# First norm of a two-layer hybrid: another order of VectorE's and ScalarE's first work, half of the squares on VectorE

## The chip, the core and the metric

One core of a Trainium2 chip runs the whole program. Its engines have queues of their own: TensorE (PE) multiplies, VectorE (DVE) and ScalarE (ACT) work elementwise, GpSimd (POOL) does a few copies, SyncE (SP) issues most DMAs. An engine takes its instructions in the order of its queue; where one waits for another engine or for a DMA, all behind it wait too. The metric is the device time of one execution in microseconds; less is better.

## The reference, cut to what matters

Two layers on a sequence of 512 tokens of width 1024, batch 1. The first is dilated attention, the second an mLSTM, each followed by a SwiGLU; a norm stands ahead of each and at the end. What this document deals with is the very beginning: the first norm and the rotary angles.

```
def rms_norm(x, g):
    xf = x.astype(jnp.float32)
    y = xf * lax.rsqrt(jnp.mean(xf * xf, axis=-1, keepdims=True) + RMS_EPS)
    return y.astype(x.dtype) * g.astype(x.dtype)

def apply_partial_rope(t, positions):
    ang = positions.astype(jnp.float32)[..., None] * inv_freq
    cos = jnp.cos(ang)[:, :, None, :]
    sin = jnp.sin(ang)[:, :, None, :]
...
h = x
h = h + dilated_attention_mixer(rms_norm(h, attn_norm[0]), positions, attn_w_in[0], attn_w_out[0])
...
proj = (xn @ w_in).reshape(B, S, N_GROUPS, 3, ATTN_HEADS, ATTN_HEAD_DIM)
```

## The kernel before

All activations are kept transposed: 128 features on the partitions, 512 tokens along a row, so x is eight tiles of 128 x 512 (KC = 8). Every matrix product is done in three passes: both operands are split into a high half, rounded to a shorter float (written by ScalarE), and a low half, the remainder (written by VectorE), and high x high, high x low and low x high are added up (SPLITS). So each tile of weights or activations costs ScalarE one instruction and VectorE one ahead of TensorE.

The norm's factor per token is not applied ahead of the first products: the products run on x times the gain, and the result is multiplied by the factor when it is taken out of PSUM. The factor's way is: squares of x summed per token (`squares`, two halves `hf` of 512 features with TB = 4 blocks of 128 tokens each, results in `ss2`), their sum `xv` (L504), a Newton inverse root, eight small diagonal blocks `xdg` (L323), and two matmuls `xbc` (L329) that spread it over the partitions. `xrbc` (L330) is that factor in SBUF; all evacuations of queries and keys need it.

The start is laid out by hand, from about L340 to L530:

- On SyncE's queue, x and the first weights come in five pieces of 1, 1, 2, 2 and 2 of the eight tiles (`pieces`), x and weights in turn, then constants, then the next weights (`a0g0k`, `a0g1q`) as their buffers come free. The positions and the gains come through ScalarE's queue.
- `x_piece(i)` splits the weights of a piece (`first_split`: `first_h` L443 on ScalarE, `first_l` L444 on VectorE), and for each tile of it transposes x on TensorE (`x_in`, `xT` L305) and splits the result times the gain (`xa_h` L226 on ScalarE, `xa_l` L227 on VectorE).
- `first_mm(i)` are the matmuls of piece i of the first product, `a0g0q` (L454).
- `gains` transposes the gains on TensorE (`arT` L428) and copies them into `cols` on VectorE (L429); every `xa_h` and `xa_l` reads them.
- `rope_turns` (L366 to L372) makes angles out of the positions on VectorE: a memset, four casts of one row each, a shuffle, two scalings. `rope_angles` (L375 to L378) reduces them to one turn. `rope_tables` takes two sines on ScalarE (L381, L382), three small steps on VectorE (L383 to L385) and eight copies on GpSimd into `sinn` and `cosn`.
- `x_keep(k)` copies the transposed x out of PSUM into `h` for the residual (VectorE for k < 4, L433; ScalarE for the rest, L435) and so frees its bank.
- `next_weights(ch)` splits the two chunks of the second product's weights (`a0g0k_k_h` L208, `a0g0k_k_l` L209).
- `idle(n)` are matmuls on ones whose result is not used; eight of them run at the start (L107).

The order on each engine is forced with `tc.issue_after(ins)`: what is traced in it goes behind `ins` in the queue of `ins`'s engine. `behind(fn, engine=E)` puts what `fn` issues on E behind E's last instruction so far (TensorE when no engine is named); `both` does it for VectorE and ScalarE at once. Where nothing is forced, the framework's scheduler settles the order when the program is built, by its own reckoning of when operands are ready; so the matmuls inside one `first_mm`, and the place of `xbc` among the matmuls of the second product `a0g0k` (L239), are its choice. `xbc` is traced after the first half of `a0g0k`.

Buffers: the tags "v" and "vf" have one buffer each; "vf" holds the angles (`tmp`) first and values later. The banks of the transposed x are handed to `a0g0k` and to the third product `a0g1q` when `x_keep` has read them.

Of the kernel before, what the change touches and what calls it, by code (L numbers as in the profile page):

```python
# [11 lines left out]
F32 = mybir.dt.float32  # L12
F32R = mybir.dt.float32r
I32 = mybir.dt.int32
AF = mybir.ActivationFunctionType
ALU = mybir.AluOpType
AX = mybir.AxisListType
P = 128
# [52 lines left out]
def tile_hybrid_dilated_attn_mlstm(  # L71
# [4 lines left out]
    nc = tc.nc  # L76
# [3 lines left out]
    def pool(stack, name, **kw):  # L80
        return stack.enter_context(tc.tile_pool(name=name, bufs=1, **kw))
# [75 lines left out]
    def last_on(engine):  # L157
        for ins in reversed(nc.cur_bb.bb.instructions):
            if ins.engine == engine:
                return ins  # L160
# [184 lines left out]
    with ExitStack() as actx:  # L345
        ap = pool(actx, "attn")
# [5 lines left out]
        part = lambda at, w: acst[:, at - K_MA:at - K_MA + w]  # L352
# [11 lines left out]
        def rope_turns():  # L364

            nc.vector.memset(n, 0.0)  # L366
            for c in range(4):
                s = slice(32 * c, 32 * c + 1)
                nc.vector.tensor_copy(n[s], posi[s].rearrange("p (j c) -> p c j", c=4)[:, c])
            nc.vector.stream_shuffle(ang, n, [0] * 32)  # L370
            nc.vector.tensor_scalar(ang, ang, cst[:, K_INV:K_INV + 1], None, op0=ALU.mult)
            nc.vector.tensor_scalar(n, ang, 1.0 / TWO_PI, ROUND, op0=ALU.mult, op1=ALU.add)  # L372
# [22 lines left out]
        xtok = ap.tile([P, TB, D], F32, tag="heads", name="x_tok")  # L395
# [18 lines left out]
        def behind(fn, *args, engine=mybir.EngineType.PE):  # L414

            with tc.issue_after(last_on(engine)):
                fn(*args)
# [40 lines left out]
        ss2 = ap.tile([P, 2, TB], F32, name="x_ss")  # L458

        def squares(hf):  # L460
            for tb in range(TB):
                sq = ap.tile([P, 512], F32, tag="v", name="x_sq")
                nc.scalar.activation(sq, xtok[:, tb, hf * 512:(hf + 1) * 512], AF.Square,
                                     accum_out=ss2[:, hf, tb:tb + 1])

        ACT, DVE = mybir.EngineType.Activation, mybir.EngineType.DVE

        def both(fn, *args):
            with tc.issue_after(last_on(ACT)):
                behind(fn, *args, engine=DVE)  # L470

        rope_turns()
        with tc.issue_after(last_on(DVE)):
            behind(gains)

        def x_piece(i):
            both(first_split, i)
            k, n = pieces[i]
            for kk in range(k, k + n):
                with tc.issue_after(last_on(ACT)), tc.issue_after(last_on(DVE)):  # L480
                    behind(x_in, kk)
        x_piece(0)
        x_piece(1)
        behind(first_mm, 0)
        x_piece(2)
        behind(first_mm, 1)
        both(x_keep, 0)
        both(x_keep, 1)
        behind(rope_angles, engine=DVE)
        x_piece(3)  # L490
        behind(first_mm, 2)
        both(rope_tables)
        both(x_keep, 2)
        both(x_keep, 3)
        x_piece(4)
        behind(squares, 0, engine=ACT)
        behind(first_mm, 3)
        def next_weights(ch):
            ready.append(split_chunk(weight_chunk(w_in, ch, D, 4, "a0g0k_k%d" % ch)))
        both(next_weights, 0)  # L500
        behind(squares, 1, engine=ACT)
        both(next_weights, 1)
        v = npl.tile([P, TB], F32, tag="rs_v4", name="xv", bufs=2)
        nc.vector.tensor_tensor(v, ss2[:, 0], ss2[:, 1], op=ALU.add)  # L504
# [632 lines left out]
    with ExitStack() as mctx:  # L1137
# [101 lines left out]
        for b in range(TB):  # L1239
            ve.scalar_tensor_tensor(fblk[32 * b:32 * b + H], blk(lf)[:, b], bias2[:, 1:2], blk(t0)[:, b],  # L1240
                                    op0=ALU.add, op1=ALU.add)
# [174 lines left out]
    with ExitStack() as fctx:  # L1416
# [47 lines left out]
        for n in range(2):  # L1464
# [27 lines left out]
            for at, tb, cs in tiles:  # L1492
# [10 lines left out]
                part = 0 if n == 0 else 1 if cs.stop < 512 else 2  # L1503
                nc.scalar.activation(junk[:, cs], t, AF.Square, accum_out=fss[:, tb, part:part + 1])
                if part == (1 if tb == TB - 1 else 0):
                    nc.vector.tensor_tensor(fpre[:, tb:tb + 1], fss[:, tb, 0:1], fss[:, tb, 1:2], op=ALU.add)
                    nc.vector.tensor_scalar(fpre[:, tb:tb + 1], fpre[:, tb:tb + 1], 1.0 / D, EPS,
                                            op0=ALU.mult, op1=ALU.add)
                nc.gpsimd.tensor_tensor(t, t, gbc[:, n * 512 + cs.start:n * 512 + cs.stop], op=ALU.mult)
                if n == 1 and cs.stop == 512:  # L1510

                    v = fv[:, tb:tb + 1]
                    nc.vector.scalar_tensor_tensor(v, fss[:, tb, 2:3], 1.0 / D, fpre[:, tb:tb + 1],
                                                   op0=ALU.mult, op1=ALU.add)
# [35 lines left out]
```

## Time and profile before

| | |
|---|---|
| median of 3 runs | 1429.59 us (1429.14 to 1430.78) |
| the profiled execution | 1429.9 us |
| its span, first to last instruction | 1427.3 us |
| mean granted TensorE clock | 0.998 |
| PE / DVE / ACT / POOL busy | 99% / 67% / 42% / 6% of the span |

A page of the profile gives busy times by engine, queues, and groups of instructions; the trace behind it can be asked for the waits of an engine, for a timeline, and for groups by line. Times in these views count from the span's start. The profiled execution is one run; the difference of 2.6 us between its time and its span lies outside its instructions.

### The profile page before, as it was taken

What the parts mean: (1) busy time and instruction counts of PE and PEld (TensorE: products, weight loads), DVE (VectorE), ACT (ScalarE), POOL (GpSimd) and SP (SyncE); (2) the same over time, 40 slices, a digit from 0 to 9 for tenths busy, and PEclk for the clock granted to TensorE, in tenths of its full rate; (3) what the DMA queues carried; (4) which work ended last, traced back from release to release, by engine and by line L of the source; (5) the groups of instructions that cost most, each with busy time, mean ns of one, the idle gap of its engine ahead of it and who ended that gap; (6) DMA issues with size and microseconds to landing.
All of it is one profiled execution on the core that took longest, in us unless ns stands there. A gap on an engine that the chain in (4) does not pass through costs nothing. (4 is left out here: it accounts for less than half of the span.)

```text
span 1427.3 us, 20249 instructions
## 1 busy us (share of the span) xinstructions
PE 1415.0 (99%) x7980; PEld 1240.0 (87%) x7980; DVE 960.3 (67%) x1680; ACT 604.1 (42%) x1010; POOL 84.9 (6%) x136
## 2 busy tenths in 40 slices
PE   8999999999999999999999999999999999999998
PEld 6888888888888888999998888888888899999887
DVE  7857557567567397787772358897758778788233
ACT  5333224224225353544462233696534354445123
POOL 1011011011002000000000010110000000002001
PEclk9999999999999999999999999999999999999999
DMA  6346236335335434323232332322133332335331
GB/s 193 102 114 202 76 104 188 100 106 153 133 104 144 146 102 133 106 73 118 90 96 96 96 98 74 104 60 60 52 113 96 125 118 83 96 119 178 118 106 72
DMA packets 134215, 158.65 MB, mean 111 GB/s; under 512 B 7076, under 2 KB 121572, under 8 KB 134120
## 3 DMA queue, kind: packets, MB, share of 16 engines
q1 hardware_dynamic: 126160, 131.55, 29.7%
q0 software_dynamic: 6288, 24.68, 6.1%
q8 instruction: 62, 1.02, 0.3%
q10 hardware_dynamic: 1672, 1.13, 0.2%
q14 instruction: 33, 0.27, 0.1%
HBM read 143.18 MB, written 14.16 MB: 110 GB/s over the span
## 5 line engine op out<-in xcount | busy, mean ns | idle before, releaser
L1479 PE MATMUL fin<-fw_l,f1hh 128*128 128x512 f32 (+1 forms) x198 | 72.5, 366 | 0.0
L1479 PE MATMUL fin<-fw_h,f1hh 128*128 128x512 f32 (+1 forms) x198 | 72.4, 366 | 0.0
L1479 PE MATMUL fin<-fw_h,f1hl 128*128 128x512 f32 (+1 forms) x198 | 72.4, 365 | 0.0
L209 DVE TENSOR_TENSOR fo_k_l<-fo_k_w,fo_k_h 128x1024 fp32r<-128x1024 f32 (+1 forms) x24 | 27.2, 1133 | 62.0 <-ACT fo_k_h L208 62.0
L239 PE MATMUL fo<-f0hh,fo_k_h 128*128 128x512 f32 x176 | 68.5, 389 | 0.0
L239 PE MATMUL fo<-f0hl,fo_k_h 128*128 128x512 f32 x176 | 68.5, 389 | 0.0
L239 PE MATMUL fo<-f0hh,fo_k_l 128*128 128x512 f32 x176 | 68.5, 389 | 0.0
L209 DVE TENSOR_TENSOR fw_l<-fw_w,fw_h 128x1024 fp32r<-128x1024 f32 x22 | 27.0, 1230 | 59.9 <-ACT fw_h L208 59.9
L208 ACT ACTIVATE fo_k_h<-fo_k_w 128x1024 fp32r<-128x1024 f32 (+1 forms) x24 | 23.7, 989 | 74.7 <-PE fo L239 74.7
L208 ACT ACTIVATE fw_h<-fw_w 128x1024 fp32r<-128x1024 f32 x22 | 23.3, 1060 | 67.3 <-PE fin L1479 67.0
L1479 PEld LDWEIGHTS fin<-fw_l,f1hh 128*128 128x128 f32 x198 | 37.4, 189 | 6.2 <-DVE fw_l L209 0.2
L1479 PEld LDWEIGHTS fin<-fw_h,f1hh 128*128 128x128 f32 x198 | 37.4, 189 | 6.2
L1479 PEld LDWEIGHTS fin<-fw_h,f1hl 128*128 128x128 f32 x198 | 37.3, 189 | 6.0
L239 PEld LDWEIGHTS fo<-f0hh,fo_k_h 128*128 128x128 f32 x176 | 33.0, 188 | 6.9
L239 PEld LDWEIGHTS fo<-f0hl,fo_k_h 128*128 128x128 f32 x176 | 33.0, 188 | 6.9
L239 PEld LDWEIGHTS fo<-f0hh,fo_k_l 128*128 128x128 f32 x176 | 33.0, 188 | 6.7
L239 PE MATMUL f0j<-n_h,f0j_h 128*128 128x512 f32 x96 | 37.5, 390 | 0.0
L239 PE MATMUL f1j<-n_h,f1j_h 128*128 128x512 f32 x96 | 37.5, 390 | 0.0
L239 PE MATMUL f0j<-n_h,f0j_l 128*128 128x512 f32 x96 | 37.4, 389 | 0.0
L239 PE MATMUL f1j<-n_h,f1j_l 128*128 128x512 f32 x96 | 37.4, 389 | 0.0
L239 PE MATMUL f0j<-n_l,f0j_h 128*128 128x512 f32 x96 | 37.3, 389 | 0.0
L239 PE MATMUL f1j<-n_l,f1j_h 128*128 128x512 f32 x96 | 37.3, 389 | 0.0
(2104 smaller groups left out, 4879.5 us busy)
## 6 DMA issues: line engine op xcount, KB each, us to landing
f0j_w<-in_ffn_w_in_dram SPq DMA_DIRECT2D x28, 512.0 KB, 5.0
f1j_w<-in_ffn_w_in_dram SPq DMA_DIRECT2D x28, 512.0 KB, 3.8
fw_w<-in_ffn_w_out_dram SPq DMA_DIRECT2D x22, 512.0 KB, 3.9
fo_k_w<-in_ffn_w_out_dram SPq DMA_DIRECT2D x20, 512.0 KB, 3.5
awo_k_w<-in_attn_w_out_dram SPq DMA_DIRECT2D x8, 512.0 KB, 6.8
mv_k_w<-in_mlstm_w_in_dram SPq DMA_DIRECT2D x8, 512.0 KB, 3.7
mqk_k_w<-in_mlstm_w_in_dram SPq DMA_DIRECT2D x8, 512.0 KB, 3.8
mo_k_w<-in_mlstm_w_in_dram SPq DMA_DIRECT2D x8, 512.0 KB, 3.6
```

Source lines behind the costliest of these rows:

```text
L208: nc.scalar.activation(hi[:, :n], raw[:, :n], AF.Copy)
L209: nc.vector.tensor_tensor(lo[:, :n], raw[:, :n], hi[:, :n].bitcast(F32), op=ALU.subtract)
L239: nc.tensor.matmul(acc, whl[a][:, k, m * P:(m + 1) * P], pairs[b][kk], start=(kk == 0 and (a, b) == SPLITS[0]), stop=(kk == nk - 1 and (a, ...
L1479: nc.tensor.matmul(acc[i][:, cs], a[a_][kk][:, tb * P:(tb + 1) * P], whl[b_][:, k, cs], start=(kk == 0 and (a_, b_) == SPLITS[0]), stop=(k ...
```

## The change

Five things are different:

- `gains` no longer stands behind `rope_turns`. Its copy goes behind VectorE's last instruction so far, which is one of the start, and its transpose is no longer put behind anything on TensorE.
- `rope_turns` is issued after `x_keep(0)` and `x_keep(1)`, just ahead of `rope_angles`, behind what VectorE has by then.
- Two more `idle` matmuls stand between the transposes of piece 0 and piece 1 in TensorE's queue.
- `x_piece(4)` is issued ahead of `x_keep(2)` and `x_keep(3)`.
- `squares(1)` runs on VectorE, between the low halves of the two chunks of `next_weights`, as four multiplications with a running sum; its scratch tile takes the buffer "vf". `squares(0)` stays on ScalarE. What is computed stays the same.

```diff
@@ -459,9 +459,13 @@
 
         def squares(hf):
             for tb in range(TB):
-                sq = ap.tile([P, 512], F32, tag="v", name="x_sq")
-                nc.scalar.activation(sq, xtok[:, tb, hf * 512:(hf + 1) * 512], AF.Square,
-                                     accum_out=ss2[:, hf, tb:tb + 1])
+                sq = ap.tile([P, 512], F32, tag=("v", "vf")[hf], name="x_sq")
+                part = xtok[:, tb, hf * 512:(hf + 1) * 512]
+                if hf == 0:
+                    nc.scalar.activation(sq, part, AF.Square, accum_out=ss2[:, hf, tb:tb + 1])
+                else:
+                    nc.vector.tensor_tensor_reduce(sq, part, part, 1.0, 0.0, op0=ALU.mult, op1=ALU.add,
+                                                   accum_out=ss2[:, hf, tb:tb + 1])
 
         ACT, DVE = mybir.EngineType.Activation, mybir.EngineType.DVE
 
@@ -469,9 +473,7 @@
             with tc.issue_after(last_on(ACT)):
                 behind(fn, *args, engine=DVE)
 
-        rope_turns()
-        with tc.issue_after(last_on(DVE)):
-            behind(gains)
+        behind(gains, engine=DVE)
 
         def x_piece(i):
             both(first_split, i)
@@ -480,25 +482,27 @@
                 with tc.issue_after(last_on(ACT)), tc.issue_after(last_on(DVE)):
                     behind(x_in, kk)
         x_piece(0)
+        behind(idle, 2)
         x_piece(1)
         behind(first_mm, 0)
         x_piece(2)
         behind(first_mm, 1)
         both(x_keep, 0)
         both(x_keep, 1)
+        behind(rope_turns, engine=DVE)
         behind(rope_angles, engine=DVE)
         x_piece(3)
         behind(first_mm, 2)
         both(rope_tables)
+        x_piece(4)
         both(x_keep, 2)
         both(x_keep, 3)
-        x_piece(4)
         behind(squares, 0, engine=ACT)
         behind(first_mm, 3)
         def next_weights(ch):
             ready.append(split_chunk(weight_chunk(w_in, ch, D, 4, "a0g0k_k%d" % ch)))
         both(next_weights, 0)
-        behind(squares, 1, engine=ACT)
+        behind(squares, 1, engine=DVE)
         both(next_weights, 1)
         v = npl.tile([P, TB], F32, tag="rs_v4", name="xv", bufs=2)
         nc.vector.tensor_tensor(v, ss2[:, 0], ss2[:, 1], op=ALU.add)
```

## The prediction

> **What bounds the kernel now.** First the page: busy times of the engines.
>
> ```profile
> span 1427.3 us, 20249 instructions
> PE 1415.0 (99%) x7980; PEld 1240.0 (87%) x7980; DVE 960.3 (67%) x1680; ACT 604.1 (42%) x1010; POOL 84.9 (6%) x136
> ```
>
> TensorE is busy 99% of the span, so an edit counts only by what it does to TensorE's waits. The change sits in the first 30 us; next, therefore, the view of waits for TensorE, from 0 to 45 us (columns: us in total, times, longest).
>
> ```profile
> PE a0g0q L454 <- DVE xa_l L227: 0.7, 1, 0.7
> PE xbc L329 <- DVE xdg L323: 0.6, 1, 0.6
> PE xT L305 <- DMA x_tok<-in_x_dram: 0.4, 1, 0.4
> PE a0g0q L454 <- ACT xa_h L226: 0.3, 1, 0.3
> ```
>
> Once x arrives TensorE waits only 2.0 us in all here: that is about the most that any reordering can win. Where each wait lies shows in the timeline, all engines (start us, duration us, engine, line, instruction, and in brackets the idle time before it and what ended it).
>
> ```profile
> 0.87 0.17 DVE L366 MEMSET angles<- 128x128 f32 x1
> ...
> 1.52 3.78 PE L107 MATMUL idle<-idle_w,ones_r 128*128 128x512 f32 x8 [1.52 <-DVE idle_w L102]
> ...
> 4.61 1.11 DVE L369 CAST angles<-posi 1x128 f32<-1x128 int32 x4 [3.15 <-DMA posi<-in_positions_dram]
> ...
> 6.44 0.23 DVE L372 TENSOR_SCALAR angles<-angles 128x128 f32<-128x128 f32 x1
> ...
> 6.59 0.16 DVE L429 COPY cols<-arT 128x8 f32<-128x8 f32 x1
> ...
> 6.84 0.69 ACT L226 ACTIVATE xa_h<-xT,cols 128x512 fp32r<-128x512 f32 x1 [1.69 <-DVE cols L429]
> ...
> 7.58 0.50 PE L454 MATMUL a0g0q<-xa_h,first_h 128*128 128x512 f32 x1 [0.34 <-ACT xa_h L226]
> ...
> 10.44 0.63 ACT L443 ACTIVATE first_h<-first_w 128x512 fp32r<-128x512 f32 x1 [2.02 <-DMA first_w<-in_attn_w_in_dram]
> ...
> 11.10 0.69 DVE L444 TENSOR_TENSOR first_l<-first_w,first_h 128x512 fp32r<-128x512 f32 x1 [1.79 <-ACT first_h L443]
> ...
> 11.96 1.09 PE L305 MATMUL xT<-cst,x_tok 128*128 128x128 f32 x8 [0.40 <-DMA x_tok<-in_x_dram]
> ...
> 13.03 1.28 DVE L433 COPY h<-xT 128x512 f32<-128x512 f32 x2
> ...
> 14.23 0.22 DVE L375 TENSOR_SCALAR angles<-angles 128x128 f32<-128x128 f32 x1
> ...
> 15.60 0.68 DVE L444 TENSOR_TENSOR first_l<-first_w,first_h 128x512 fp32r<-128x512 f32 x1
> ...
> 15.72 0.31 ACT L381 ACTIVATE angles<-angles 128x128 f32<-128x128 f32 x1 [1.24 <-DVE angles L378]
> ...
> 16.20 1.40 DVE L227 SCALAR_TENSOR_TENSOR xa_l<-xT,cols,xa_h 128x512 fp32r<-128x512 f32 x2
> ...
> 18.18 1.28 DVE L433 COPY h<-xT 128x512 f32<-128x512 f32 x2
> ...
> 19.98 1.40 DVE L227 SCALAR_TENSOR_TENSOR xa_l<-xT,cols,xa_h 128x512 fp32r<-128x512 f32 x2
> ...
> 20.69 1.04 ACT L208 ACTIVATE a0g0k_k_h<-a0g0k_k_w 128x1024 fp32r<-128x1024 f32 x1
> 20.77 0.50 PE L454 MATMUL a0g0q<-xa_l,first_h 128*128 128x512 f32 x1 [0.74 <-DVE xa_l L227]
> ...
> 21.77 1.23 DVE L209 TENSOR_TENSOR a0g0k_k_l<-a0g0k_k_w,a0g0k_k_h 128x1024 fp32r<-128x1024 f32 x1 [0.39 <-ACT a0g0k_k_h L208]
> ...
> 23.17 0.39 PE L239 MATMUL a0g0k<-xa_h,a0g0k_k_h 128*128 128x512 f32 x1
> ```
>
> Three regimes are to be seen. Up to 11.96 data sets the pace: ScalarE idles 2.02 us for weight piece 2, VectorE idles 1.79 us behind that, TensorE waits for x. From 11.10 to 21.4 VectorE works without a hole and its low halves (xa_l) reach TensorE last. From 23.17 TensorE runs on.
>
> **The change, part by part.** *The gains come first.* In the rows before, the copy of the gains (6.59) stands behind the four casts (4.61) and the chain up to 6.44, so ScalarE's first xa_h waits 1.69 us for it. Now that copy can run when its transpose is done. The first product of 7.58 moves up by at most the 1.98 us from 4.61 to 6.59. It is worth nothing: the matmuls after it only wait longer for x at 11.96, and VectorE still cannot start piece 2 before 11.10, because ScalarE waits for its weights until 10.44.
>
> *Two idle matmuls.* The first eight take 3.78 us, so two take about 0.95 us or less. They lie where TensorE waits anyway for x piece 1 and for the first xa_h. If that cover were gone they would push the first product back by up to 0.95, and the hole before 11.96 (0.40) would take up part of that. I book 0.
>
> *The turns (L366 to L372) go behind the first two copies of h.* There VectorE has no hole. From the first cast at 4.61 to the end of the last one (6.44 + 0.23) are 2.06 us; the next instruction needs its result, and the memset (0.17) is now in the same queue: 2.3 us in all. The angles then start at 14.23 + 2.3 = 16.5 instead of 14.23. Queued behind them on VectorE are piece 3 (15.60 to 17.9, its xa_l 16.20 to 18.5) and on ScalarE the two sines (15.72 to 18.0). Bounds: 2.0 if the casts run closer together, 2.5 with more waiting.
>
> *Piece 4 passes the copies of h 2 and 3.* These copies (1.28, 1.20 start to start) leave the way of the last low halves: these start at 19.98 + 2.3 - 1.2 = 21.1. The copies then end near 23.6; the second product's accumulators take over those banks, which TensorE reaches later.
>
> *ScalarE's queue then decides.* Behind the sines stand piece 4's weights, two xa_h, four squares and the first weights of the second product, all in the order of before. The last starts at 20.69, which is 4.97 behind the sine; 18.0 + 4.97 = 23.0, done 1.04 later at 24.0. TensorE's second product, at 23.17 before, can start at 24.05: +0.9. TensorE itself would be ready sooner or about then: its order was laid out with products of high halves ahead of those that need xa_l, and if nothing is laid out anew (the first late xa_l costs 2.3 in full, the 0.74 wait at 20.77 and the hidden rest come off) it is there 1.2 later. So +0.9 to +1.2. The low half of those weights follows at 24.05 + 1.23 = 25.3, and TensorE's third matmul wants it at 24.5; the order of products can hide this (0) or not (0.8). I take 0 here, since the next term covers it.
>
> *Half of the squares go to VectorE.* The price of one such instruction with a sum isn't in the trace at this size; the view of lines by form gives neighbours.
>
> ```profile
> L444 DVE TENSOR_TENSOR first_l<-first_w,first_h 128x512 fp32r<-128x512 f32 x3 | 2.1, 684 | 1.8 <-ACT first_h L443 1.8
> L589 DVE CUSTOM_DVE_ANT_0 a0p<-a0s,acst 128x256 f32<-128x256 f32 x6 | 2.3, 411 | 0.0
> ```
>
> From below 0.60 us (15.60 to 16.20, start to start, no sum to read), from above 0.82 (two of the 256-wide ones, which do sum). The four write one buffer in turn and so can't overlap: 0.75 each, 3.0 in all (2.4 to 3.3). What follows on VectorE and TensorE:
>
> ```profile
> 24.65 0.16 DVE L504 TENSOR_TENSOR xv<-x_ss 128x4 f32<-128x4 f32 x1 [1.66 <-ACT x_sq L463]
> ...
> 25.74 1.22 DVE L209 TENSOR_TENSOR a0g0k_k_l<-a0g0k_k_w,a0g0k_k_h 128x1024 fp32r<-128x1024 f32 x1
> ...
> 28.54 1.65 DVE L323 TENSOR_SCALAR xdg<-cst,xrhl 128x128 fp32r<-128x128 f32 x8
> ...
> 37.23 0.72 DVE L543 STREAM_SHUFFLE rot<-a0g0k 32x512 f32<-32x512 f32 x1
> ...
> 42.55 1.28 DVE L549 TENSOR_TENSOR a0g_k<-a0g_k,rot 32x512 f32<-32x512 f32 x2
> ```
>
> ```profile
> 28.61 0.39 PE L239 MATMUL a0g0k<-xa_h,a0g0k_k_h 128*128 128x512 f32 x1
> 29.55 0.47 PE L329 MATMUL xbc<-xdg,ones_r 128*128 128x512 f32 x1 [0.55 <-DVE xdg L323]
> ```
>
> ```profile
> 38.53 0.39 PE L239 MATMUL a0g1q<-xa_h,a0g1q_k_h 128*128 128x512 f32 x1
> ...
> 46.37 3.28 PE L583 MATMUL a0s<-a0g_k,a0g_q 128*128 128x128 f32 x16
> ```
>
> VectorE's 1.66 us wait for ScalarE's squares goes away, but not its end: low half of the first weights to 25.2, squares to 28.2, low half of the second weights (1.14 start to start, 21.77's 1.23 less the overlap) to 29.4, then the norm. From xv to xdg the trace has 28.54 - 24.65 = 3.89, in it about 1.02 for the weights that cut in at 25.74: 2.87. So xdg starts near 32.3 instead of 28.54: 3.75 later. The two xbc matmuls wait for it. They have a fixed place in TensorE's queue, laid out by the scheduler when it reckons xdg to be ready: before, one matmul behind the first 24 of the second product (23.17 to 28.61, 0.227 each). If it lays k further matmuls ahead of xbc, TensorE passes that point 3.75 - 0.227 k later than before. Its reckoning sees the same added instructions, so k should be about (2.9 to 3.75, less its own delay of 0.6 to 0.9) / 0.227, 8 to 13; it was somewhat early before too (the 0.55 wait). I take k = 10: +1.5 in all, and this includes the +0.9 and the low half of the weights.
>
> *Later on VectorE's lag meets two slacks.* The rotated q and k end at 43.83, their scores start at 46.37: 2.54 of slack against 3.75, so +1.2 is enough. The bank that the shuffle of 37.23 frees is taken at 38.53: 0.58 of slack, but the scheduler has ten more matmuls of the other half (2.3) to put ahead. Neither asks for more than 1.5.
>
> **Sum.** 0 (gains) + 0 (idle) + 1.5. The profiled execution took 1429.9 us, 2.6 around its span of 1427.3; it becomes 1431.4. It stands 0.3 above the median of the runs shown (1429.59), where the sum gives 1431.1. I say 1431.2.
>
> **Rivals.** (1) *xbc is laid too early.* VectorE's added work costs more than the scheduler reckons (narrow casts, sums), k is 0 to 5: +3.75 to +2.6, time 1432.2 to 1433.4, about 1433. For it: it was already too early before. Against: it put the products of high halves ahead by itself. (2) *Not slower.* The place is the sines. If TensorE and ScalarE get there no later than now, the 0.74 at 20.77 and the wait at xbc can be won: TensorE's floor from x at 11.96 is near 22.0 for the second product (16 transposes in about 1.7 and 36 matmuls at 0.227, without a hole), -1.1 at best, time 1428.5 to 1429.6, about 1429.3. It decides from a delay of the sines below 2.3 - 0.9 = 1.4; it would need the turns to cost 1.4 in place of 2.1 to 2.3, or the squares on VectorE to let the norm end in time. Against: the casts in the row are 0.28 each, and nothing suggests that they waited on one another. (3) *The clock falls.* With k = 0 TensorE idles some 3 us ahead of xbc. The eight idle matmuls at the start (0.47 each, against 0.227 later) show a slow clock at first; if such a hole brought it back for a stretch as long as the hole, the matmuls there would cost 1.5 to 3 more: +5.3 to +6.8, about 1435.5. No hole of that length stands in this trace's middle.
>
> [...]
>
> **How the numbers follow.** Forecast 0.45 (1430.5 to 1432.0), rival 1 0.34, rival 2 0.13, rival 3 and changes of order far behind 0.08. The bound of 0.2% is 2.9 us, to about 1432.5, about what a measurement of this kernel can tell from no change: of rival 1 some four fifths lie above it, 0.27, with rival 3 and a bit of the forecast 0.37 slower; faster by 2.9 is beyond what the waits hold, 0.03; 0.60 within. The range reaches over rival 1 and into rival 2: 1429.4 to 1434.0.
>
> **What would show it.** Right, if the sines start near 18.0, the second product near 24, xdg near 32.3 and xbc with a wait of 0.5 to 1.5 us. The gains are right if the first product comes sooner and the transposes still wait at 11.96. Wrong, if sines start before 17 (turns cheaper), if xdg starts before 31 (squares cheaper), or if xbc waits over 2.5 us (rival 1). If TensorE's waits up to 50 us add up to about what they were and the time still differs, the cause lies behind this stage.

## The result, and the profile after

| | before | changed |
|---|---|---|
| median | 1429.70 us (1429.00 to 1430.99, 8 runs) | 1434.74 us (1433.26 to 1436.76, 8 runs) |
| ratio of the two | | 1.0034, 95% interval 1.0023 to 1.0045 |
| profiled execution / its span | 1429.9 / 1427.3 us | 1436.76 / 1433.6 us |

The change makes the kernel 5.0 us slower. 1431.2 was forecast, with a range to 1434.0: the direction is right, the size is not. The page of the changed kernel, first line and busy times:

```profile
span 1433.6 us, 20254 instructions
PE 1417.4 (99%) x7982; PEld 1241.7 (87%) x7982; DVE 963.2 (67%) x1688; ACT 601.4 (42%) x1002; POOL 85.2 (6%) x136
```

VectorE has eight instructions more (four squares, four readings of their sums) and 2.9 us more of busy time; ScalarE has eight fewer and 2.7 us less. TensorE has two matmuls more, but 2.4 us more of busy time: most of that cannot be the two, which take 1.14 us at 6.20. The view of TensorE's waits, changed kernel, 0 to 60 us (us in total, times, longest):

```profile
PE a0g1k L239 <- DVE a0g1k_k_l L209: 2.5, 1, 2.5
PE a0g0q L454 <- DVE xa_l L227: 2.1, 1, 2.1
...
PE xbc L329 <- DVE xdg L323: 0.4, 1, 0.4
PE xT L305 <- DMA x_tok<-in_x_dram: 0.2, 1, 0.2
```

The second and third rows are the places that the prediction dealt with. The first is a place that it did not name: the product `a0g1k`, at 54 us, waits for the low half of its weights.

**In this execution the front came out nearly as worked out.** The timeline of the changed kernel (start us, duration us, engine, line, instruction; in brackets the idle time before it):

```profile
13.89 0.17 DVE L366 MEMSET angles<- 128x128 f32 x1
...
17.57 0.68 DVE L444 TENSOR_TENSOR first_l<-first_w,first_h 128x512 fp32r<-128x512 f32 x1
17.69 0.31 ACT L381 ACTIVATE angles<-angles 128x128 f32<-128x128 f32 x1 [3.62 <-DVE angles L378]
...
18.97 0.50 PE L454 MATMUL a0g0q<-xa_l,first_h 128*128 128x512 f32 x1 [2.14 <-DVE xa_l L227]
...
22.66 1.99 ACT L208 ACTIVATE a0g0k_k_h<-a0g0k_k_w 128x1024 fp32r<-128x1024 f32 x2
...
23.73 1.23 DVE L209 TENSOR_TENSOR a0g0k_k_l<-a0g0k_k_w,a0g0k_k_h 128x1024 fp32r<-128x1024 f32 x1 [0.39 <-ACT a0g0k_k_h L208]
...
24.09 0.39 PE L239 MATMUL a0g0k<-xa_h,a0g0k_k_h 128*128 128x512 f32 x1
...
25.60 0.69 DVE L467 CUSTOM_DVE_ANT_0 x_sq<-x_tok 128x512 f32<-128x512 f32 x1
...
28.82 0.16 DVE L508 TENSOR_TENSOR xv<-x_ss 128x4 f32<-128x4 f32 x1
...
31.68 1.66 DVE L323 TENSOR_SCALAR xdg<-cst,xrhl 128x128 fp32r<-128x128 f32 x8
...
32.70 0.47 PE L329 MATMUL xbc<-xdg,ones_r 128*128 128x512 f32 x1 [0.36 <-DVE xdg L323]
```

The sines start at 17.69 (18.0 forecast), the second product at 24.09 (24.05), `xdg` at 31.68 (32.3), and `xbc` waits 0.36 (0.5 to 1.5). Up to the first `a0g1k` matmul, at 50.20 instead of 49.30, TensorE has lost 0.90 us in all.

That is one execution. A second profiled execution of the same kernel took 1434.21 us (span 1432.4). Its hole ahead of the first late `xa_l` is about as long, 2.18 us, but over the 4 us that follow the granted clock is 0.57 (third number from the end of the first row; the other columns are explained below), and the second product starts at 26.55, 3.4 later than before:

```profile
20.00:24.00 4.00, 4.00 (x11) 3.13 (x12) 3.96 (x9) 3.90 (x11) 2.82 (x8) 0.57 0.25 73
```

```profile
26.55 0.39 PE L239 MATMUL a0g0k<-xa_h,a0g0k_k_h 128*128 128x512 f32 x1
```

**The rest is lost behind it.** VectorE's queue around the two evacuations of `a0g1q` (L740), first in the kernel before:

```profile
43.76 0.67 DVE L740 TENSOR_TENSOR a0g_q<-a0g1q,xrbc 128x512 f32<-128x512 f32 x1
...
44.99 1.20 DVE L209 TENSOR_TENSOR a0g1k_k_l<-a0g1k_k_w,a0g1k_k_h 128x1024 fp32r<-128x1024 f32 x1
...
46.43 0.69 DVE L740 TENSOR_TENSOR a0g_q<-a0g1q,xrbc 128x512 f32<-128x512 f32 x1 [0.25 <-PE a0g1q L239]
...
47.75 0.27 DVE L589 CUSTOM_DVE_ANT_0 a0p<-a0s,acst 128x128 f32<-128x128 f32 x1
...
49.30 0.59 PE L239 MATMUL a0g1k<-xa_h,a0g1k_k_h 128*128 128x512 f32 x1
...
49.97 0.40 PE L239 MATMUL a0g1k<-xa_h,a0g1k_k_l 128*128 128x512 f32 x1
```

and in the changed one (the same evacuation is L744, the score reductions L593):

```profile
46.89 0.67 DVE L744 TENSOR_TENSOR a0g_q<-a0g1q,xrbc 128x512 f32<-128x512 f32 x1
...
48.14 0.66 DVE L744 TENSOR_TENSOR a0g_q<-a0g1q,xrbc 128x512 f32<-128x512 f32 x1
...
49.43 0.27 DVE L593 CUSTOM_DVE_ANT_0 a0p<-a0s,acst 128x128 f32<-128x128 f32 x1
...
50.20 0.58 PE L239 MATMUL a0g1k<-xa_h,a0g1k_k_h 128*128 128x512 f32 x1
...
51.65 0.41 DVE L593 CUSTOM_DVE_ANT_0 a0p<-a0s,acst 128x256 f32<-128x256 f32 x1
51.66 0.40 PE L239 MATMUL a0g2q<-xa_l,a0g2q_k_h 128*128 128x512 f32 x1
...
53.27 1.21 DVE L209 TENSOR_TENSOR a0g1k_k_l<-a0g1k_k_w,a0g1k_k_h 128x1024 fp32r<-128x1024 f32 x1
...
54.54 0.50 PE L239 MATMUL a0g1k<-xa_h,a0g1k_k_l 128*128 128x512 f32 x1 [2.48 <-DVE a0g1k_k_l L209]
...
56.11 0.63 PE L239 MATMUL a0g1k<-xa_h,a0g1k_k_h 128*128 128x512 f32 x1
...
56.54 0.63 PE L239 MATMUL a0g1k<-xa_l,a0g1k_k_h 128*128 128x512 f32 x1
...
59.44 0.39 PE L239 MATMUL a0g1k<-xa_h,a0g1k_k_h 128*128 128x512 f32 x1
```

Before, the low half `a0g1k_k_l` (44.99) lies between the two evacuations and is long done when TensorE wants it at 49.97. In the changed kernel it lies behind the second evacuation, the eight score reductions (49.43 to 52.06) and a rotation: 53.27. TensorE does what it can without it, two matmuls of a later product too (51.66), then idles 2.48 us. This is an order in VectorE's queue, settled when the program is built, and no mere lag: the evacuation is 3.1 us late, the low half 8.3.

After the hole the matmuls start 0.43 us apart (56.11, 56.54) instead of 0.23. The view of stretches (from : to, length, busy times of PE, its weight loads, VectorE, ScalarE, GpSimd; then the granted clock, DMA share, GB/s):

```profile
52.00:54.00 2.00, 0.05 (x1) 0.00 (x0) 2.00 (x6) 1.82 (x8) 0.00 (x0) 1.00 0.00 0
54.00:56.00 2.00, 1.46 (x4) 1.23 (x5) 2.00 (x4) 2.00 (x10) 0.00 (x0) 0.73 0.12 25
56.00:58.00 2.00, 2.00 (x6) 1.52 (x6) 2.00 (x2) 0.01 (x1) 0.00 (x0) 0.50 0.74 241
58.00:60.00 2.00, 2.00 (x10) 1.61 (x9) 0.03 (x1) 0.00 (x0) 0.00 (x0) 0.92 0.87 267
```

The granted clock falls to 0.50 and is back by 60 us; some eight matmuls cost 0.20 more each, 1.6 us. Hole (2.65, counted from where the next matmul would have started) and clock make 4.3 us: behind them TensorE is 5.2 behind the kernel before. The span of this one execution is 1.1 more; most of that is a wait at about 150 us:

```profile
150.21 1.83 PE L717 MATMUL a0o<-a0pT,a0v 128*128 128x128 f32 x14 [0.86 <-DMA a0pT<-a0pD]
```

The second profiled execution does not show this wait, and is the nearer one to the median. In the profiles of the experiments it comes back at that size once, with 1.0 us in e8, so it is no mark of the change.

### The profile page after: what moved, and what is told of

It is laid out like the page before. It is cut to its first block, busy times and chain, and to the rows that moved or that the text cites. A ratio compares the mean times of both kernels' runs of the same rounds, so it can differ in the third digit from the quotient of the medians.

```text
span 1433.6 us, 20254 instructions
## 1 busy us (share of the span) xinstructions
PE 1417.4 (99%) x7982; PEld 1241.7 (87%) x7982; DVE 963.2 (67%) x1688; ACT 601.4 (42%) x1002; POOL 85.2 (6%) x136
```

## The experiments

Two theories stand against each other at first. In the expectations of e1, e2, e3 and e5, A is that the place of that low half, with the hole and the clock that follow, makes the loss beyond the forecast; B puts the loss into the front, the squares or VectorE's lag. The expectations of the later runs say what A and B are there. All ratios are against the kernel before on the same chip.

| run | what it is | median us | ratio, 95% interval |
|---|---|---|---|
| e1 | changed, all squares on ScalarE | 1433.57 | 1.0028 (1.0017 to 1.0038) |
| e2 | changed, turns at the start again | 1432.62 | 1.0020 (1.0011 to 1.0029) |
| e3 | changed, low half ahead again | 1431.23 | 1.0013 (1.0004 to 1.0022) |
| e4 | changed, hole filled | 1433.19 | 1.0025 (1.0015 to 1.0034) |
| e5 | before, low half behind | 1431.53 | 1.0015 (1.0006 to 1.0024) |
| e6 | e3, front hole filled | 1430.43 | 1.0007 (0.9998 to 1.0016) |
| e7 | turns in holes, piece 4 ahead | 1430.57 | 1.0009 (1.0000 to 1.0018) |
| e8 | e7, low half ahead, one square on VectorE | 1427.86 | 0.9990 (0.9981 to 0.9999) |
| e9 | e2, low half ahead | 1428.54 | 0.9991 (0.9982 to 1.0000) |
| e10 | e6, all squares on ScalarE | 1430.90 | 1.0009 (1.0000 to 1.0017) |
| e11 | before, piece 4 ahead alone | 1432.12 | 1.0017 (1.0008 to 1.0026) |
| e12 | before, squares on VectorE alone | 1431.76 | 1.0017 (1.0007 to 1.0026) |
| e13 | before, later turns alone | 1431.84 | 1.0015 (1.0007 to 1.0024) |

The medians of the kernel before in these runs are 1429.27 (e1 to e4), 1429.35 (e5, e6, e8), 1429.53 (e7, e9, e10) and 1429.58 (e11 to e13). Differences below are against these.

### The squares back (e1), the turns back (e2)

```diff
...
-        behind(squares, 1, engine=DVE)
+        behind(squares, 1, engine=ACT)
```

> The changed kernel with all eight squares on ScalarE again; turns, gains, idle matmuls and the order of piece 4 stay changed. Theory A (VectorE's queue: the first low half of a0g1k stands behind the score reductions, TensorE stalls on it at about 52 us, and a slow clock follows): that half stays behind the reductions here too, but VectorE reaches the reductions about 1.7 us sooner (48 instead of 49.4), so the half is ready near 52.7 instead of 54.5. Second product starts at +0.9 as with the change, the stall at a0g1k shrinks from 2.65 to about 0.8, no slow matmuls behind it: 1.7 to 2.0 over before, about 1431.5. Theory B (what is lost is the wait ahead of xa_l at the start, 2.1 us, and some of it is paid again later): the start is unchanged, so the time stays near 1434.5.

1433.57: between the two. The low half still lies behind the reductions, with a hole of 1.75 us (A expected 0.8) and a granted clock of 1.00 after it (50 to 60 us). What neither expectation had is the front: after the hole at the first late `xa_l` the clock fell in this profile (0.85 over the 10 us from 20 to 30), and the second product starts 3.0 late instead of 0.9.

```diff
-        behind(gains, engine=DVE)
+        rope_turns()
+        with tc.issue_after(last_on(DVE)):
+            behind(gains)
...
-        behind(rope_turns, engine=DVE)
```

> The changed kernel with the turns back at the start, ahead of the gains, as before; half of the squares stay on VectorE. Theory A: the second product starts no later than before (23.2 or up to 1 us sooner), but the squares still make VectorE some 2.5 us late, the first low half of a0g1k still stands behind the score reductions and is ready near 53.2; TensorE stalls there for 2 to 3 us, and about 1.7 us of slow clock may follow: 2 to 4 over before, 1431.7 to 1433.7. Theory B: the wait ahead of xa_l is gone, so the time is that of before or up to 1 us less, 1428.7 to 1429.7.

1432.62, as A has it. The second product starts 0.78 *earlier* than before the change, TensorE does not wait for the late `xa_l`, and all is lost at `a0g1k`: a hole of 2.29 us, and the granted clock behind it (0.83 over the 10 us from 50 to 60).

### The low half ahead (e3), the hole filled (e4)

e3 traces the first low half of `a0g1k` behind the first evacuation of `a0g1q`; nothing else is different from the changed kernel.

```diff
...
                         rope_part(sh, m, acc)
+                        if pr == 0 and g == 1 and part == 0 and m == 0:
+                            ready.append(split_chunk(weight_chunk(w_in, 0, 4 * D, 4, "a0g1k_k0")))
```

> The changed kernel, all its parts kept; only the first weights of a0g1k are split ahead of the second evacuation of a0g1q, where VectorE did this before the change, and not behind the score reductions. Theory A: the stall at a0g1k and the slow matmuls behind it go away; what is left is the second product's +0.9: 0.9 to 1.2 over before, about 1430.8 (up to 1431.8 if the transposed probabilities still land late once at about 150 us). Theory B: the front is unchanged, so the time stays near 1434.5.

1431.23: 3.1 of the 5.0 us are gone with one instruction's place. In the timeline of e3 it lies between the evacuations, though these are still later than in the changed kernel's profile:

```profile
47.61 0.67 DVE L744 TENSOR_TENSOR a0g_q<-a0g1q,xrbc 128x512 f32<-128x512 f32 x1
48.84 1.20 DVE L209 TENSOR_TENSOR a0g1k_k_l<-a0g1k_k_w,a0g1k_k_h 128x1024 fp32r<-128x1024 f32 x1
49.97 0.67 DVE L744 TENSOR_TENSOR a0g_q<-a0g1q,xrbc 128x512 f32<-128x512 f32 x1
```

So VectorE's lag alone makes no hole here. What is left over is in front; the stretch of e3 behind its 2.20 us hole there:

```profile
20.00:24.00 4.00, 4.00 (x13) 3.15 (x12) 3.66 (x8) 3.91 (x11) 2.81 (x8) 0.61 0.39 123
```

e4 leaves the order of the changed kernel and adds nine matmuls, whose result is not used, behind the first scores.

```diff
+            def keep_busy():
+                hot = ps.tile([P, 512], F32, tag="t", name="hot", bufs=1)
+                for i in range(9):
+                    nc.tensor.matmul(hot, ones_r, pair[0][i % KC], start=True, stop=True)
...
```

> The changed kernel with nine more matmuls whose result is not used (2.05 us at full speed) behind the first scores, in front of a0g1k, so that TensorE has work in most of the hole of 2.65 us. The low half that TensorE waits for comes when it came. If the hole itself slows TensorE's clock, a0g1k's matmuls after it run at 0.227 us each at once and not at 0.43, the shift of everything behind is about 3.5 in place of 5.2, time about 1433.0, 1.7 less than the changed kernel. If the 0.43 us come from something else at that place (VectorE's or DMA's traffic), the matmuls there stay slow and the time stays near 1434.7.

1433.19, and the matmuls after the filled stretch start 0.23 apart, at a granted clock of 1.00 (50 to 60 us). The low half is as late as before, so this parts the loss: 1.1 us for the clock (5.04 less 3.92), the other 2.0 for the time that TensorE truly lacks its operand.

### The same place in the kernel before (e5)

```diff
...
+                        if pr == 0 and g == 1 and part == 1:
+                            chunk = weight_chunk(w_in, 0, base + part * D, 4, "a0g1k_k0")
+                            with tc.issue_after(scored[0, 1]):
+                                ready.append(split_chunk(chunk))
```

`scored[0, 1]` is VectorE's last instruction of the score reductions.

> The kernel before, with one thing of the changed kernel's order and none of its edits: the first weights of a0g1k are split behind the score reductions on VectorE. Theory A (the place of this split is most of the loss): the start is as before; the half starts near 51.7 instead of 44.99 and is done near 52.9, TensorE has six matmuls to do from 49.3 and then idles about 2.0 us; everything behind is about 2.1 later, and up to 2 more where the hole lets the clock fall: 1431.3 to 1433.2. Theory B (the start carries the loss): as before, 1429.3.

1431.53: 2.2 us from an order alone, with an undisturbed front. The wait in its profile, and the clock after it:

```profile
PE a0g1k L239 <- DVE a0g1k_k_l L209: 1.8, 1, 1.8
```

```profile
54.00:56.00 2.00, 2.00 (x6) 1.56 (x6) 2.00 (x4) 0.52 (x3) 0.00 (x0) 0.54 0.83 261
```

This profiled execution is one of the two slowest of the eleven (1434.78; the nine others lie below 1432.5), and its span is 1431.1 us. Six of the others have spans of 1429.1 to 1429.7, about what the hole alone adds to the 1427.4 of the kernel before. So after 1.75 us of idling the clock seems to fall in some executions only; the profiles with such holes, in the last section, bear that out.

### The front hole filled (e6), and without the squares (e10)

e6 is e3 with eight matmuls, whose result is not used, ahead of the transposes of tile 6, where TensorE idles.

```diff
+            if k == 6:
+                for i in range(8):
+                    nc.tensor.matmul(tp, ones_r, pair[0][i % 4], start=True, stop=True)
```

> The kernel with the split ahead, and eight matmuls without use in front of the transposes of tile 6, which the first late xa_l leaves time for: the hole of 2.3 us at about 17 us is left at about 0.5. In the profiles with the turns moved a0g0q's matmuls behind that hole took 0.43 us each for about 4 us in three of four. If the hole is what slows the clock, they run at 0.23 here, the second product starts at +0.9 to +1.1 in place of +2.8, and the time is about 1430.3, 0.9 less than with the split ahead alone (1431.2). If something else slows them, nothing changes: 1431.2.

1430.43, and no slow clock in its profile (1.00 in every stretch from 10 to 70 us): it was worth about 0.9 in front (1.96 less 1.08). The second product starts at 24.74, 1.6 later than before, where 0.9 to 1.1 was expected. e10 takes the squares back to ScalarE as e1 did.

> The changed kernel with the low half ahead and the front hole filled with eight unused matmuls, and all eight squares on ScalarE again; what is left is the later turns alone. Theory A (the rest of 1.1 us over the kernel before comes from the front: sines, piece 4's weights and the second product's weights late): second product +1.2 to +1.6 as with the squares on VectorE, 1430.0 to 1430.9 us. Theory B (the rest comes from the squares on VectorE): 1429.2 to 1429.7.

1430.90, as A has it: +1.37 against +1.08. The two intervals overlap, so no cost of the squares on VectorE is to be seen once the low half has its place; what is left comes with the later turns.

### The squares without the turns, the low half ahead (e9)

> The changed kernel with the turns at the start again and with the first low half of a0g1k ahead of the second evacuation; of the change, the half of the squares on VectorE (and piece 4 ahead of two copies of h) is left. Theory A (the squares on VectorE cost only by pushing that low half behind the score reductions, and the hole and the slower clock that follow): no hole at a0g1k, 1428.7 to 1430.0 us, against 1432.62 with the turns at the start alone. Theory B (the 3 us of squares cost of themselves, by the late norm and xbc): 1430.8 or more.

1428.54, a little below A's range and 1.0 *under* the kernel before; its interval just reaches 1. The timeline of e9:

```profile
18.72 1.40 DVE L227 SCALAR_TENSOR_TENSOR xa_l<-xT,cols,xa_h 128x512 fp32r<-128x512 f32 x2
...
22.06 0.39 PE L239 MATMUL a0g0k<-xa_h,a0g0k_k_h 128*128 128x512 f32 x1
```

Piece 4 has passed two copies of `h`, so the last `xa_l` start at 18.72 instead of 19.98. The 0.74 us for which TensorE waited there (20.77 in the prediction's rows) is gone, and the second product starts 1.1 sooner. This gain was inside the change all along; how much of it is the squares' was not taken apart.

### Each part alone (e11, e12, e13)

```diff
         both(rope_tables)
+        x_piece(4)
         both(x_keep, 2)
         both(x_keep, 3)
-        x_piece(4)
```

> The kernel before with piece 4 ahead of the two copies of h alone. Built so, the first low half of a0g1k stands behind the score reductions, though VectorE has no more work than before. Theory A (this part alone is enough to lose the place, which costs 2 to 2.5, and wins the 0.7 of TensorE's wait for xa_l): a hole of 1.5 to 2.3 us at a0g1k, 1430.0 to 1431.6 us. Theory B (the place matters only when VectorE's work has grown): no such hole, 1428.5 to 1429.0.

1432.12, above A's 1431.6. VectorE has not one instruction more here, yet the low half starts at 51.83, behind the reductions. TensorE's waits in e11:

```profile
PE a0g1k L239 <- DVE a0g1k_k_l L209: 1.8, 1, 1.8
...
PE xT L305 <- DMA x_tok<-in_x_dram: 1.3, 1, 1.3
```

The wait for `xa_l` is gone, as in e9, but in this execution x itself arrived late (the second row; 0.4 before), so nothing was won. Whether that holds in the other runs isn't shown.

e12 keeps of the change the squares on VectorE, the two idle matmuls and neither move. The gains stand behind the turns again, as before; its expectation is wrong in calling them changed.

> The kernel before with half of the squares on VectorE, gains and the idle matmuls as changed, and neither the later turns nor piece 4 ahead. Built so, the first low half of a0g1k stands behind the score reductions as well. Theory A: a hole of 2 to 2.6 us there, xbc waits about as before, no 0.7 won at xa_l: 1431.3 to 1433.5 us. Theory B (squares are free and the place harmless): 1429.2 to 1430.2.

1431.76: the same place lost, a hole of 1.75 us, a little shorter than A's; in its profile the clock fell behind it (0.50 from 54 to 56 us). `xbc` waits 0.8 instead of 0.6, and `a0g1k` starts 0.14 late. e13 keeps the later turns, the gains and the idle matmuls.

> The kernel before with the later turns (and gains and idle matmuls as changed), squares on ScalarE, piece 4 where it was. Built so, the first low half of a0g1k stays ahead of the second evacuation. Theory A (the turns cost by the front alone): no hole at a0g1k; the last xa_l come 2.3 later, front wait 2 to 3 us, second product +1.2 to +3, 1430.5 to 1432.5 us. Theory B (the turns are hidden, most of the change's loss is the place): 1429.0 to 1429.8.

1431.84, as A has it. Here the low half stays between the evacuations (47.09, between 45.85 and 48.52), and all is lost in front. TensorE's wait in e13, and the stretch behind it:

```profile
PE a0g0q L454 <- DVE xa_l L227: 2.2, 1, 2.2
```

```profile
20.00:24.00 4.00, 4.00 (x12) 3.13 (x11) 3.59 (x8) 3.91 (x11) 2.67 (x8) 0.57 0.14 33
```

So the squares, and the earlier piece 4, each suffice to lose the place; the turns don't. Why the scheduler's reckoning tips over in these two stays open: no run shows that reckoning. That VectorE's queue was tight is no answer, since in e11 it had no more to do.

### A better version (e7, e8)

e7, from the kernel before: gains first; the memset at the start; the four casts behind the first `first_l`, the shuffle and scalings behind the second piece's `xa_l`, where VectorE idles; piece 4 ahead of the two copies. e8 adds the edit of e3 and one of the eight squares on VectorE.

```diff
+            if i == 0:
+                behind(rope_turns, engine=DVE)
...
         x_piece(1)
+        behind(rope_spread, engine=DVE)
```

> The kernel before with gains first, the turns laid in two pieces into VectorE's holes behind pieces 0 and 1, piece 4 ahead of two copies of h, all squares on ScalarE, and the low half of a0g1k left where the scheduler puts it, which in this program is behind the eight score reductions. Theory A (that order costs some 2 us wherever it arises): a hole of 1.5 to 2.3 us at a0g1k, 1429.8 to 1431.5 us, against 1427.86 with the low half ahead. Theory B (it hurts only with a late front): no hole over 0.5 us, 1427.9 to 1428.6.

> A version put together from what the traces show: from the kernel before, the gains first; the turns in VectorE's early holes (casts behind the first low weights, shuffle and scalings behind the second xa_l); piece 4 ahead of the copies of h; one square of eight on VectorE; the first weights of a0g1k split ahead of the second evacuation of a0g1q. Theory A: no late xa_l, the second product starts near 22.0 (1.2 sooner than before), no hole at a0g1k: 0.8 to 1.3 less than before, about 1428.2. If VectorE's load and not its order decided (theory B), the square costs and the time is 1429.3 to 1430.

1430.57 and 1427.86. e7 starts the second product 0.9 sooner than before and idles 1.75 us at `a0g1k`, where the low half fell behind once more:

```profile
PE a0g1k L239 <- DVE a0g1k_k_l L209: 1.8, 1, 1.8
```

e8 has no hole there. It is 1.5 us faster than before, and by that 6.5 faster than the changed kernel; its interval ends just below 1. Its one profile is of the slowest of its eleven executions (1429.54); there the second product starts at 22.73, not near 22.0 as expected.

## Why the prediction was wrong, point by point

- *Gains first, idle matmuls: 0.* Right in size. The copy of the gains ran at 5.54, when its transpose was done, and the first product started at 7.53 instead of 7.58. One sign did not come: the transposes that were to go on waiting at 11.96 ran from 11.67 without a wait.
- *Turns 2.3, sines 18.0, second product 24.05.* The first two are right: memset to the last scaling is 13.89 to 16.15 (2.26), sines 17.69. The 24.09 of the second product is right by another way than the one named first, and partly by luck. ScalarE did not decide: its chain took the 4.97 us worked out (17.69 to 22.66), VectorE could take up the result at 23.73, and TensorE came 0.36 later from its own hole of 2.14 us, without waiting. In the five other profiles with the later turns and that hole left open (the second of the changed kernel, e1, e3, e4, e13) the granted clock fell behind it (0.57 to 0.85 over 4 to 10 us, in the last section), and the second product started at 25.87 to 26.55.
- *Squares 0.75 each, xdg 32.3, k = 10.* Right: 24.87, 25.60, 26.33, 27.07 are 0.735 apart; 3.1 of the 3.75 forecast for `xdg`; 35 matmuls of the second product stand ahead of `xbc` instead of 25 (the quotient that k was taken from comes to 9 to 14, not 8 to 13). The wait of `xbc`, 0.36, is below the 0.5 named as a sign, and TensorE is 0.90 late when it reaches `a0g1k`. The sum of +1.5 for this stage stands against +1.08 (e6, no slow clock) and +1.96 (e3, with it).
- *"Later on VectorE's lag meets two slacks", "Neither asks for more than 1.5".* This step failed. The two slacks held: no matmul waits at either place in the changed kernel. But the step listed who waits for VectorE's lag in the order of the kernel before, and took that order for given, though the paragraph above it let the same scheduler lay `xbc` anew. So all that lies behind the front was put at nothing. A third customer stood between the two evacuations, the low half of 44.99, with no rule that held it there. Its new place costs 3.1 us (e3), or 2.2 in the kernel before (e5), and two parts of the change bring it about alone (e11, e12). Reading the VectorE rows from 43 to 52 us for what has no forced order would have shown that nothing holds it, though not that it would move.
- *Rival 3, the clock.* What it supposed was seen, at another place and after a shorter hole than its 3 us: a granted clock of 0.50 behind the 2.48 us of the changed kernel. The slow stretch was not as long as the hole, though: about 1.7 us of clock were lost after 1.75 us as after 2.48. And the 0.47 us of the first matmuls, from which it argued, go with a granted clock of 1.00 (0 to 5 us, kernel before). The 2.3 for the first late `xa_l` was in the prediction's own numbers, and 2.14 came. So the sum took a slow clock in front at nothing, though a hole stood there; no run had shown how long a hole must be. The slow clock costs about 1.1 at `a0g1k` (e4) and 0.9 in front (e6).
- *Rival 2, not slower.* It named the sines as the deciding place, and that is borne out: with the turns at the start and the low half ahead (e9) the rest of the change is 1.0 faster, near the 1.1 that it gave as the most, and the second product starts at 22.06, the floor that it reckoned near 22.0.

The medians, put together: the turns cost 2.1 (1.08 + 0.99, e6 against e9) and their slow clock 0.9; the lost place 2.0 and its slow clock 1.1; piece 4 and the squares win 1.0 once the place is kept. That makes the 5.0. It does so by the way it was taken, since each run differs from the next by one of these steps; each term is a difference of medians from separate runs, good to a few tenths.

## What to carry to other kernels

Where a scheduler fills gaps by itself, list what it has put into a gap without being told to, and fix that place by hand before anything upstream is moved: here one low half out of place cost 3.1 us, and all the rest of the change 2.0. Judge a bundle of edits part by part; here piece 4 ahead and the squares on VectorE win 1.0 us together, and this was hidden under the later turns and the lost place. On a TensorE-bound kernel price a hole of 2 us at up to twice its length (2.48 us of hole made 4.3 us of delay here), and fill it with spare matmuls if it can't be closed (that won 1.1 in e4 and 0.9 in e6).

## What the runs showed of the hardware

**The clock falls after short holes, and not always.** The holes of these profiles, from the end of one matmul to the start of the next: 2.48 (changed, `a0g1k`), 2.29 (e2), 2.20 (e3, e4, in front), 2.19 (e1, in front), 2.18 (second profile of the changed kernel, front) and 2.17 us (e13) were each followed by a lower granted clock: 0.50 over 2 us in the changed kernel, 0.57 to 0.61 over 4 us in its second profile, e3 and e13, 0.83 to 0.85 over 10 us in e1, e2 and e4. 2.14 (changed, front) and 2.03 (second profile, `a0g1k`) were followed by 1.00; of five of 1.75 us two by a lower one (0.54 in e5 and 0.50 in e12, over 2 us) and three by 1.00 (e1, e7, e11). A hole of 1.68 us near 960 us, ahead of a transpose of the second layer (`m1yT`), left the clock at 1.00 in the kernel before and in the changed one. In e5 and e13 the slow spell began only after work had resumed: the stretch in which the hole ends still reads 1.00 (52 to 54 and 16 to 20 us), the next one 0.54 and 0.57.

**The slow spells lose the same time.** In each of the nine profiles that have one, the clock lost adds up to about 1.7 us (1.68 to 1.72 by the stretches), whether the hole was 1.75 or 2.48 us long. The stretches of the changed kernel above give it: 2 us each at 0.73, 0.50 and 0.92 are 0.54, 1.00 and 0.16 lost. 0.50 is also the lowest that a stretch of 2 us shows elsewhere (e12); at 0.50 throughout, 1.7 us lost make a spell of some 3.4 us, an estimate from these two numbers. Of the 14 holes of 1.75 us and more listed here 9 were followed by a lower clock; what decides it is not shown by these runs. The first 12 us are left out here: the eight idle matmuls at the start take 0.47 us each in the kernel before and in the changed one, at a granted clock of 1.00, and these views don't show why.
